# Sums of weight and activation tiles made by accumulating transfers instead of VectorE

## The chip, the cores and the metric

The kernel runs on one core of one Trainium2 chip. The metric is the device time of one execution in microseconds, as the median of repeated runs. The core has five engines with queues of their own: TensorE (PE), VectorE (DVE), ScalarE (ACT), GpSimd (POOL) and SyncE (SP), which issues transfers.

## The reference

Two layers over 1024 tokens of width 1024, all in float32. Layer 0 mixes by sliding-window attention, layer 1 by a gated linear recurrence; each is followed by a squared-ReLU block with an inner width of 4096.

```python
def sqrelu_mlp(h, w_up, w_down):
    return jnp.square(jax.nn.relu(h @ w_up)) @ w_down

for layer in range(DEPTH):
    h = rmsnorm(x, mix_norm[layer])
    y = sliding_window_attention(h, ...) if layer % N_MIXERS == 0 else hgrn2_recurrence(h, ...)
    x = x + y
    h = rmsnorm(x, mlp_norm[layer])
    x = x + sqrelu_mlp(h, mlp_w_up[layer], mlp_w_down[layer])
return rmsnorm(x, final_norm)
```

The recurrence begins with `q, f, i, g = split(h @ w_in, 4)`, four projections of 1024 by 1024.

## The kernel before, in words

All activations are held transposed, as tiles of 128 features by 512 tokens (256 KB in float32; a "half" `hf` is 512 tokens). A float32 product is made of three matmuls: each operand is split into a rounded part and a rest (`split` and `weight_split`, lines 402 and 419: a cast on ScalarE or VectorE, then a subtraction on VectorE), and `mm3` (line 384) multiplies high by high, high by low and low by high.

The up and down matrices of both layers and the four projections of the recurrence use a seven-product scheme (Strassen's, in Winograd's form). Weight and activation are cut in quarters; products 1 and 2 take plain quarters, products 3 to 7 take sums and differences of quarters on one side or both. So three kinds of sums are made, all on VectorE before the change:

- Sums of activations that stay on the chip: `begin` and `finish` (lines 508 and 516) make the seven right-hand sides of 4 tiles each once per layer. They stay on VectorE.
- Sums of weights for up and recurrence: `strassen_weights` (line 567) loads the four quarters of one group and makes four sums in "m" tiles, then splits seven tiles into "wh" and "wl" tiles. `pair` (line 581) runs the seven products for two inner tiles of the up matrix, 16 pairs per layer; `two` (line 1058) does it for two projections, twice for each of the 8 heads.
- Sums for down: `operands` (line 626) makes, for one inner tile pair `p` of 16, the weight and the activation of one product. The activations come back from HBM, where `square_relu` (line 486) had put them (`hid`). `T[p]` and `S[p]` are running sums that are kept in "a" tiles from product to product.

`down` (line 661) runs six passes over all 16 `p`: products 1 and 5, then 6, 7, 4, 2 and 3. In a pass a product of one `p` is 12 matmuls of 512 columns (4 output tiles, 3 matmuls each). Operands are asked for two steps of `p` ahead.

The order of the work is made by a planner (`Schedule`, line 140). The code says which operations there are, in which they read and write; each has a rank (its place in the code, moved ahead by `lead`), a cost and, for transfers, a tail. The planner plays the five engines forward with these costs and writes each engine's queue; a buffer of a tag ("wr" 5, "wh" 5, "wl" 5, "m" 7, "t" 18, "a" 60) is handed on when its last user has ended in that play. On the chip each queue is then worked off in order, with semaphores between the engines. Every instruction is issued by `call`, so all have one line in the profile (326 before), and groups are told apart by the tags of their tiles: `wl<-m,wh` is the rest of a split of an "m" tile.

Of the kernel before, what the change touches and what calls it, by code (L numbers as in the profile page):

```python
# [277 lines left out]
class Net:  # L278
    def __init__(self, ctx, tc, io):
# [10 lines left out]
        self.ones = self.const((P, P))  # L290
        self.memset(self.ones, 1.0)
        self.mean = self.const((P, 1))
        self.memset(self.mean, 1.0 / D)
# [102 lines left out]

    def raw(self, src):
        r = self.tile("wr", BUFS["wr"], (P, TH), F32)
        self.dma(r, src, 4 * P * TH)
        return r  # L400
# [95 lines left out]
    def gained(self, which, kt, hf):  # L496

        u = self.t()
        self.act(u, self.x[kt][hf], AF.Copy, scale=self.gain(which, kt))
        return u  # L500
# [7 lines left out]
    def begin(self, which):  # L508

        self.b, self.u = {k: [] for k in range(1, 8)}, []  # L510
        for kt in range(KT):
            u = self.gained(which, kt, 0)
            self.b[1 + kt // HK].append(self.split(u))
            self.u.append(self.keep(u))

    def finish(self, which, upper_first=False):

        x, t, q01, q11 = self.b, [], [], []

        def stored(j):  # L520
            z = self.t()
            self.dma(z, self.u[j], 4 * P * TH)
            return z

        def lower():
            for j in range(HK):
                q01.append(self.gained(which, j, 1))
                t.append(stored(j))
                self.tt("any", t[j], q01[j], t[j], ALU.subtract)
                x[5].append(self.split(t[j]))  # L530

        def upper():
            for j in range(HK):
                q11.append(self.gained(which, j + HK, 1))
                x[3].append(self.split(q11[j]))

        for part in (upper, lower) if upper_first else (lower, upper):
            part()
        for j in range(HK):
            self.tt("any", t[j], q11[j], t[j], ALU.subtract)  # L540
            x[6].append(self.split(t[j]))
        for j in range(HK):
            self.tt("any", q01[j], q11[j], q01[j], ALU.subtract)
            x[7].append(self.split(q01[j]))
        for j in range(HK):
            z = stored(j + HK)
            self.tt("any", z, z, t[j], ALU.subtract)
            x[4].append(self.split(z))
        return x
# [17 lines left out]
    def strassen_weights(self, first, second, done=()):  # L567

        self.s.lead = LEAD
        a = {(i, k): self.raw(src[:, k * TH : k * TH + TH]) for i, src in enumerate((first, second)) for k in range(2)}  # L570
# [5 lines left out]
        order = ((1, a[0, 0]), (5, s1), (2, a[0, 1]), (6, s2), (3, s4), (7, s3), (4, a[1, 1]))  # L576
        w = {name: self.weight_split(z) for name, z in order if name not in done}
        self.s.lead = 0
# [41 lines left out]

    def hidden(self, i, hf, p):
        z = self.t()
        self.dma(z, self.hid[p + i * MT // 2, hf], 4 * P * TH)
        return z

    def operands(self, name, p, T, S, held=False):

        a = lambda i, k: self.raw(self.io["down"][self.layer, k, p, :, i])
        h = lambda i, hf: self.hidden(i, hf, p)

        def sum_of(tile, x, y, alu=ALU.subtract):
            self.tt("any", tile, x, y, alu)
            return tile

        if name == 1:
            self.corner = a(0, 0), h(0, 0)
            w, x = self.corner
        elif name == 5:
            first, q00 = self.corner
            T[p] = x = sum_of(self.a(), h(0, 1), q00)  # L640
            w = sum_of(self.t(tag="m"), a(1, 0), a(1, 1), ALU.add)
        elif name == 6:
            T[p] = x = sum_of(T[p], h(1, 1), T[p])
            w = S[p]
        elif name == 7:
            x = sum_of(self.t(), h(1, 1), h(0, 1))
            w = sum_of(self.t(tag="m"), a(0, 0), a(1, 0))
        elif name == 4:
            x = sum_of(T[p], h(1, 0), T[p])
            w = a(1, 1)  # L650
        elif name == 2:
            w, x = a(0, 1), h(1, 0)
        else:
            x = h(1, 1)
            w = sum_of(S[p], a(0, 1), S[p])
        got = self.split(w) if held else self.weight_split(w), self.split(x)
        if name == 5:
            S[p] = sum_of(self.a(), w, first)
        return got

    def down(self, cut):
# [31 lines left out]

        def scaled_sum(hf, out, z, tokens=slice(0, TH)):

# [3 lines left out]
            part = out[:, tokens].only(tokens.start)  # L699
            self.tt("any", part, u, part, ALU.add, k)  # L700

# [23 lines left out]
        for i in range(2):  # L725
            for m in range(HK):
                z = residual(m + (1 - i) * HK, 1)
                scaled_sum(1, z, y[1 - i, 1, m])
                self.x[m + (1 - i) * HK][1] = z
        run_pass((4,))  # L730
        for m in range(HK):
            z = residual(m + HK, 0)
            scaled_sum(0, z, main[m])
            self.x[m + HK][0] = z
# [311 lines left out]
    def two_first(self, which, e, x):  # L1046
# [5 lines left out]
        self.product(main, w[0], x[1], True)  # L1052
        self.copy(y0, main)
        self.product(own, w[1], x[2], True)
        self.tt("DVE", y0, own, y0, ALU.add)
        return main, y0

    def two(self, which, e, x, out, begun=None):
# [6 lines left out]
        if not begun:  # L1065
            self.product(main, w[1], x[1], True)
            self.copy(y0, main)
        yield
# [3 lines left out]
        self.product(main, w[6], x[6], False)  # L1072
        self.copy(y1, main)
        yield
        if not begun:
            self.product(own, w[2], x[2], True)
            self.tt("DVE", y0, own, y0, ALU.add)
        yield
# [3 lines left out]
        self.product(side, w[3], x[3], False)  # L1082
        self.tt("DVE", y1, side, y1, ALU.add)
        yield
# [290 lines left out]
```

## Time and profile before

| | |
|---|---|
| median of 3 runs | 2181.79 us (2180.43 to 2184.33) |
| profiled execution, first to last instruction | 2174.9 us |
| PE busy | 2129.5 us (98%) |
| VectorE busy | 1823.6 us (84%) |
| ScalarE busy | 837.7 us (39%) |
| GpSimd busy | 62.4 us (3%) |
| HBM read and written | 250.39 MB and 63.96 MB, 145 GB/s over the span |

The span is of one profiled execution; what lies before the first and behind the last instruction is not in it, and the profile gives no time of its own for that execution beside the span. The stages by the rows of the trace: attention to about 342 us, the up stage of layer 0 to 653, its down stage to about 966, the recurrence with the changes of layer around it to about 1533, the second up stage to 1844, the second down stage to 2157, then the final norm.

"Busy" of PE counts matmuls that overlap in a pipeline, so a busy PE is not one at its peak; what counts is whether the next matmul had to wait. In a group's row the last columns are the busy time, the mean of one in nanoseconds, and the time that the engine stood idle just before them with what ended it. In a row of stretches there are the busy times of PE, its weight loads, DVE, ACT and POOL with their counts, the granted TensorE clock, the share of the 16 DMA engines that was busy, and the GB/s that they moved. Tile names are the tags above; `in_down` and `in_up` are weights in HBM, `d` is scratch in HBM, `p` and `q` are PSUM.

### The profile page before, as it was taken

What the parts mean: (1) busy time and instruction counts of PE and PEld (TensorE: products, weight loads), DVE (VectorE), ACT (ScalarE), POOL (GpSimd) and SP (SyncE); (2) the same over time, 40 slices, a digit from 0 to 9 for tenths busy, and PEclk for the clock granted to TensorE, in tenths of its full rate; (3) what the DMA queues carried; (4) which work ended last, traced back from release to release, by engine and by line L of the source; (5) the groups of instructions that cost most, each with busy time, mean ns of one, the idle gap of its engine ahead of it and who ended that gap; (6) DMA issues with size and microseconds to landing.
All of it is one profiled execution on the core that took longest, in us unless ns stands there. A gap on an engine that the chain in (4) does not pass through costs nothing.

```text
span 2174.9 us, 32278 instructions
## 1 busy us (share of the span) xinstructions
PE 2129.5 (98%) x11374; PEld 1713.3 (79%) x11374; DVE 1823.6 (84%) x3608; ACT 837.7 (39%) x1757; POOL 62.4 (3%) x124
## 2 busy tenths in 40 slices
PE   8999999999999999999999999999999999999997
PEld 6777778888877887877788888878788887888786
DVE  8899889667789888899888888878976678988887
ACT  5567755122234233365333333343521223322442
POOL 4030000000000000000100000000000000000000
PEclk9999999999999999999999999999999999999999
DMA  6212363333369867741111111547333336976652
GB/s 204 75 48 83 112 194 116 105 109 111 108 204 305 274 202 234 247 136 49 56 57 59 58 53 52 188 148 227 113 114 103 107 116 224 305 241 226 209 171 78
DMA packets 174274, 316.49 MB, mean 146 GB/s; under 512 B 19616, under 2 KB 21664, under 8 KB 174112
## 3 DMA queue, kind: packets, MB, share of 16 engines
q1 hardware_dynamic: 174112, 314.43, 44.7%
q8 instruction: 89, 1.46, 0.3%
q14 instruction: 73, 0.60, 0.1%
HBM read 250.39 MB, written 63.96 MB: 145 GB/s over the span
## 4 chain that ended last, share of the span: by engine, by line
PE 85%; DVE 7%; ACT 4%; DMA 2%; issue 1%; SPq 0%; DVEq 0%; ACTq 0%
PE q L326 45%; PE p L326 40%; DVE a L326 3%; DVE t L326 2%; ACT t L326 1%; ACT a L326 1%; DVE wl L326 1%; DVE m L326 1%; DMA wr<-in_down 1%; ACT m L326 1%; ACT wh L326 0%; DMA t<-d 0%; DVE wh L326 0%; DMA d<-t 0%; DMA a<-d 0%
## 5 line engine op out<-in xcount | busy, mean ns | idle before, releaser
L326 PE MATMUL q<-a,wh 128*128 128x512 f32 x2560 | 798.6, 395 | 5.0 <-DVE t L326 2.3
L326 PE MATMUL p<-a,wh 128*128 128x512 f32 x2336 | 754.4, 402 | 9.1 <-ACT t L326 3.7
L326 PEld LDWEIGHTS q<-a,wh 128*128 128x128 f32 x2560 | 480.1, 188 | 120.5 <-ACT t L326 4.1
L326 PEld LDWEIGHTS p<-a,wh 128*128 128x128 f32 x2336 | 432.0, 189 | 107.7 <-ACT t L326 4.6
L326 PE MATMUL q<-a,wl 128*128 128x512 f32 x1280 | 499.5, 394 | 0.0
L326 PE MATMUL p<-a,wl 128*128 128x512 f32 x1168 | 462.8, 397 | 0.0
L326 PEld LDWEIGHTS q<-a,wl 128*128 128x128 f32 x1280 | 240.4, 188 | 56.6
L326 PEld LDWEIGHTS p<-a,wl 128*128 128x128 f32 x1168 | 220.4, 189 | 50.5 <-issue 0.5
L326 DVE TENSOR_TENSOR wl<-wr,wh 128x512 fp32r<-128x512 f32 x352 | 241.0, 686 | 15.5 <-ACT wh L326 5.4
L326 ACT COPY t<-q 128x512 f32<-128x512 f32 (+2 forms) x201 | 111.8, 562 | 349.0 <-PE q L326 344.1
L326 DVE TENSOR_TENSOR a<-t,a 128x512 fp32r<-128x512 f32 (+1 forms) x294 | 195.0, 685 | 0.8 <-DMA t<-d 0.5
L326 DVE CAST wh<-wr 128x512 fp32r<-128x512 f32 x204 | 87.8, 430 | 127.6 <-PE p L326 78.4
L326 DVE TENSOR_TENSOR wl<-m,wh 128x512 fp32r<-128x512 f32 x256 | 176.3, 689 | 16.1 <-ACT wh L326 6.1
L326 ACT CAST wh<-m 128x512 fp32r<-128x512 f32 x153 | 95.2, 623 | 210.4 <-PE q L326 148.4
L326 DVE TENSOR_TENSOR t<-t,t 128x512 f32<-128x512 f32 (+3 forms) x268 | 159.7, 611 | 17.7 <-DMA t<-d 10.7
L326 ACT CAST a<-t 128x512 fp32r<-128x512 f32 x189 | 114.7, 619 | 128.8 <-PE q L326 82.6
L326 ACT CAST wh<-wr 128x512 fp32r<-128x512 f32 x148 | 91.1, 619 | 172.7 <-PE p L326 109.3
L326 PE MATMUL p<-wh,a 128*128 128x512 f32 x384 | 130.6, 407 | 8.2 <-ACT a L326 7.0
L326 DVE TENSOR_TENSOR m<-wr,wr 128x512 f32<-128x512 f32 x160 | 109.7, 687 | 22.2 <-DMA wr<-in_down 11.9
L326 PEld LDWEIGHTS q<-t,t 128*64 128x64 f32 (+1 forms) x2160 | 98.0, 144 | 25.0 <-issue 11.2
L326 PE MATMUL q<-t,t 128*64 128x32 f32 (+2 forms) x2160 | 111.5, 230 | 0.0
L326 DVE CAST wh<-m 128x512 fp32r<-128x512 f32 x103 | 44.3, 430 | 73.4 <-PE q L326 59.7
(117 smaller groups left out, 2113.9 us busy)
## 6 DMA issues: line engine op xcount, KB each, us to landing
t<-d SPq DMA_DIRECT2D x296, 256.0 KB, 4.7
wr<-in_down SPq DMA_DIRECT2D x256, 256.0 KB, 3.9
d<-t SPq DMA_DIRECT2D x180, 256.0 KB, 2.4
wr<-in_up SPq DMA_DIRECT2D x128, 256.0 KB, 2.9
wr<-in_win SPq DMA_DIRECT2D x68, 256.0 KB, 2.9
a<-d SPq DMA_DIRECT2D x60, 256.0 KB, 4.4
wr<-in_wqkv SPq DMA_DIRECT2D x48, 256.0 KB, 2.8
d<-a SPq DMA_DIRECT2D x48, 256.0 KB, 2.4
```

The source lines that it names most:

```text
L326: fn(*[place(a) for a in args], **{k: place(v) for k, v in kw.items()})
```

## The change

All weight sums of `strassen_weights` and all weight and activation sums of `operands` are made by transfers that GpSimd issues with `accum_op=ALU.add`: the source tile in HBM is added to a tile in SBUF that a plain transfer of SyncE had filled. In a group of weights `rows` becomes a10 + a11, then takes a00, then a01, and between the additions it is split for products 5, 6 and 3; `column` is a00 and takes a10 for product 7. In a down stage `S[p]` and `T[p]` are built in the same way over the passes, and product 7 has a pair of its own in an "m" and a "t" tile.

[...] So that all sums are additions, two quarters of the inner activations are stored negated (`square_relu` for the lower half of the inner tiles), as are two quarters of the right-hand sides (`begin`, `finish`); the splits of products 2 and 6 negate again, and signs turn where results are gathered.

```diff
+    def accumulate(self, out, in_, nbytes):
+
+        self.op("Pool", self.nc.gpsimd.dma_start, [out], [in_, out], 1100.0, out, in_, accum_op=ALU.add, tail=2500.0)
...
-    def split(self, src, new=None):
+    def split(self, src, new=None, negative=False):
         hi, lo = ((new or self.a)(F32R) for _ in range(2))
+        if negative:
+            self.act(hi, src, AF.Copy, scale=-1.0)
+            self.stt(lo, src, -1.0, hi.bitcast(F32), ALU.mult, ALU.subtract)
+            return hi, lo
...
     def square_relu(self, m, hf, c, psum):
-        r = self.t()
-        if psum:
+        r, lower = self.t(), m < MT // 2
+        if lower and not hf:
+            self.stt(r, c, 0.0, c, ALU.min, ALU.mult)
+        elif lower:
+            self.act(r, c, AF.Relu, scale=-1.0)
+            self.stt(r, c, 0.0, r, ALU.min, ALU.mult)
+        elif psum:
             self.act(r, c, AF.Relu)
-            self.stt(r, c, 0.0, r, ALU.max, ALU.mult)
+            self.stt(r, r, -1.0, r, ALU.mult, ALU.mult)
...
     def strassen_weights(self, first, second, done=()):
...
-        s1, s2, s3, s4 = (self.t(tag="m") for _ in range(4))
-        self.tt("any", s1, a[1, 0], a[1, 1], ALU.add)
-        self.tt("any", s2, s1, a[0, 0], ALU.subtract)
-        self.tt("any", s3, a[0, 0], a[1, 0], ALU.subtract)
-        self.tt("any", s4, a[0, 1], s2, ALU.subtract)
...
+        rows, column = self.raw(a[1, 0], "m"), self.raw(a[0, 0], "m")
+        self.accumulate(rows, a[1, 1], 4 * P * TH)
...
+        made(1, column)
+        made(5, rows)
+        if 2 not in done:
+            made(2, self.raw(a[0, 1]))
+        self.accumulate(rows, a[0, 0], 4 * P * TH)
+        made(6, rows)
+        self.accumulate(rows, a[0, 1], 4 * P * TH)
+        made(3, rows)
+        self.accumulate(column, a[1, 0], 4 * P * TH)
+        made(7, column)
+        made(4, self.raw(a[1, 1]))
...
         if name == 1:
-            self.corner = a(0, 0), h(0, 0)
-            w, x = self.corner
+            w, x = self.raw(a(0, 0)), self.hidden(0, 0, p)
         elif name == 5:
-            first, q00 = self.corner
-            T[p] = x = sum_of(self.a(), h(0, 1), q00)
-            w = sum_of(self.t(tag="m"), a(1, 0), a(1, 1), ALU.add)
+            T[p] = x = more_x(self.hidden(0, 1, p, self.a), 0, 0)
+            S[p] = self.a()
+            self.dma(S[p], a(1, 0), 4 * P * TH)
+            w = more_w(S[p], 1, 1)
         elif name == 6:
-            T[p] = x = sum_of(T[p], h(1, 1), T[p])
-            w = S[p]
+            w, x = more_w(S[p], 0, 0), more_x(T[p], 1, 1)
         elif name == 7:
-            x = sum_of(self.t(), h(1, 1), h(0, 1))
-            w = sum_of(self.t(tag="m"), a(0, 0), a(1, 0))
+            x = more_x(self.hidden(1, 1, p), 0, 1)
+            w = more_w(self.raw(a(0, 0), "m"), 1, 0)
         elif name == 4:
-            x = sum_of(T[p], h(1, 0), T[p])
-            w = a(1, 1)
+            w, x = self.raw(a(1, 1)), more_x(T[p], 1, 0)
...
-            x = h(1, 1)
-            w = sum_of(S[p], a(0, 1), S[p])
-        got = self.split(w) if held else self.weight_split(w), self.split(x)
-        if name == 5:
-            S[p] = sum_of(self.a(), w, first)
-        return got
+            w, x = more_w(S[p], 0, 1), self.hidden(1, 1, p)
+        return self.split(w) if held else self.weight_split(w), self.split(x, negative=name in (2, 6))
```

TensorE has the same matmuls as before. In GpSimd's queue there was no transfer before. Between the last small operation of the attention and the first of the recurrence, where the first up and down stage lie, nothing stood:

```order
L326 TENSOR_SCALAR m_2842<-c_243 128x4
L326 TENSOR_SCALAR m_2896<-c_243 128x4
L326 TENSOR_SCALAR m_2958<-c_243 128x4
L326 TENSOR_SCALAR m_3105<-c_243 128x4
L326 IOTA t_9647 128x64
```

Now the same queue at the place in the first down stage where product 7 is next. Its rows `a<-d` here add to the `T` tiles for product 4, `a<-in_down` to the `S` tiles for product 3, and `m<-in_down` to the weights of product 7:

```order
L328 DMA a_7189<-d_6540 128x512
L328 DMA a_6957<-in_down 128x512
L328 DMA a_7259<-d_6794 128x512
L328 DMA a_7039<-in_down 128x512
L328 DMA a_7135<-in_down 128x512
L328 DMA a_7200<-in_down 128x512
L328 DMA a_7270<-in_down 128x512
L328 DMA m_7850<-in_down 128x512
L328 DMA m_7874<-in_down 128x512
```

All 32 accumulations for the later products 4 and 3 stand ahead of the last nine weight sums of product 7; seven others of product 7 stand earlier, five of them among those of the up stage.

VectorE's queue in the first down stage before (`m<-wr,wr` is a sum of weights, `a<-m,wr` the running sum `S`, `a<-t,a` with a `T` tile or the rest of a split, `wl` the rest of a weight's split):

```order
L326 TENSOR_TENSOR wl_6820<-wr_6555,wh_6798 128x512
L326 TENSOR_TENSOR m_6828<-wr_6762,wr_6771 128x512
L326 TENSOR_TENSOR a_6838<-a_6796,a_6815 128x512
L326 TENSOR_TENSOR wl_6847<-m_6677,wh_6831 128x512
L326 TENSOR_TENSOR a_6852<-m_6828,wr_6738 128x512
L326 TENSOR_TENSOR a_6861<-t_6658,a_6705 128x512
```

And in the first down stage of the changed kernel:

```order
L328 CAST a_6796<-a_6684 128x512
L328 TENSOR_TENSOR wl_6801<-a_6578,wh_6785 128x512
L328 TENSOR_TENSOR a_6808<-a_6684,a_6796 128x512
L328 CAST wh_6817<-wr_6461 128x512
L328 CAST a_6821<-a_6733 128x512
L328 TENSOR_TENSOR wl_6828<-wr_6461,wh_6817 128x512
L328 TENSOR_TENSOR a_6834<-a_6733,a_6821 128x512
```

The sums are gone from it; what is left are the splits, and those of `S` and `T` tiles (`a_6578`, `a_6684`, `a_6733`) now follow a transfer of GpSimd.

More of the change, by code (lines that the diff above doesn't have):

```diff
@@ L395, in gain, with neg_gain, raw @@
         return self.par[:, which * KT + kt : which * KT + kt + 1]
-    def raw(self, src):
-        r = self.tile("wr", BUFS["wr"], (P, TH), F32)
+    def neg_gain(self, which, kt):
+        return self.neg_par[:, which * KT + kt : which * KT + kt + 1]
+    def raw(self, src, tag="wr"):
+        r = self.tile(tag, BUFS[tag], (P, TH), F32)
         self.dma(r, src, 4 * P * TH)
@@ L692, in run_pass, with scaled_sum @@
             return ws
-        def scaled_sum(hf, out, z, tokens=slice(0, TH)):
+        def scaled_sum(hf, out, z, tokens=slice(0, TH), add=True):
             k = tokens.stop - tokens.start
@@ L699, in scaled_sum @@
             part = out[:, tokens].only(tokens.start)
-            self.tt("any", part, u, part, ALU.add, k)
+            self.tt("any", part, part, u, ALU.add if add else ALU.subtract, k)
         def residual(m, hf):
@@ L1052, in two_first @@
         self.product(main, w[0], x[1], True)
-        self.copy(y0, main)
+        self.act(y0, main, AF.Copy, scale=-1.0)
         self.product(own, w[1], x[2], True)
-        self.tt("DVE", y0, own, y0, ALU.add)
+        self.tt("DVE", y0, y0, own, ALU.subtract)
         return main, y0
@@ L1076, in two @@
             self.product(own, w[2], x[2], True)
-            self.tt("DVE", y0, own, y0, ALU.add)
+            self.tt("DVE", y0, y0, own, ALU.subtract)
         yield
@@ L1082, in two @@
         self.product(side, w[3], x[3], False)
-        self.tt("DVE", y1, side, y1, ALU.add)
+        self.tt("DVE", y1, y1, side, ALU.subtract)
         yield
```

50 lines of the change are left out of this document (28 added, 22 removed).

## The prediction

> **What bounds the kernel now.** I read the page first: engines, DMA queues, then the chain of work that ended last.
>
> ```profile
> span 2174.9 us, 32278 instructions
> ...
> PE 2129.5 (98%) x11374; PEld 1713.3 (79%) x11374; DVE 1823.6 (84%) x3608; ACT 837.7 (39%) x1757; POOL 62.4 (3%) x124
> ...
> q1 hardware_dynamic: 174112, 314.43, 44.7%
> ...
> PE 85%; DVE 7%; ACT 4%; DMA 2%; issue 1%; SPq 0%; DVEq 0%; ACTq 0%
> ...
> L326 DVE TENSOR_TENSOR m<-wr,wr 128x512 f32<-128x512 f32 x160 | 109.7, 687 | 22.2 <-DMA wr<-in_down 11.9
> ```
>
> The chain is TensorE for 85% and VectorE for 7%. VectorE is busy (84%) but mostly beside TensorE. A busy PE need not be a full one, so the second view is the chain in order of time. A piece of it from the first up stage (columns: start, length, what):
>
> ```profile
> 383.66 16.67 PE q L326 x72
> ```
>
> 72 matmuls of 512 columns in 16.67 us are 0.232 us each, with nothing between. The third view cuts the span into stages (columns: busy time of PE, PEld, DVE, ACT, POOL, granted clock, DMA share, GB/s). The first three down rows are the passes for products 1 and 5, for 6, and for 7:
>
> ```profile
> 342.00:653.00 311.00, 310.96 (x1343) 251.19 (x1342) 234.22 (x406) 79.07 (x141) 0.00 (x0) 1.00 0.39 125
> 653.00:742.00 89.00, 88.16 (x382) 71.19 (x381) 82.28 (x138) 33.39 (x58) 0.00 (x0) 1.00 0.92 304
> 742.00:787.00 45.00, 45.00 (x196) 36.52 (x195) 36.75 (x67) 11.42 (x20) 0.00 (x0) 1.00 0.47 148
> 787.00:832.00 45.00, 44.71 (x194) 35.85 (x193) 41.28 (x71) 16.08 (x30) 0.00 (x0) 1.00 0.86 292
> ...
> 921.00:966.00 45.00, 41.79 (x174) 33.52 (x173) 40.49 (x99) 28.48 (x53) 0.36 (x2) 0.92 0.49 158
> 966.00:1010.00 44.00, 40.70 (x170) 31.85 (x169) 41.51 (x79) 26.17 (x48) 0.00 (x0) 0.96 0.17 58
> 1010.00:1490.00 480.00, 475.93 (x3866) 384.22 (x3865) 418.28 (x955) 177.04 (x364) 9.70 (x18) 1.00 0.29 92
> ...
> 1844.00:1933.00 89.00, 87.56 (x378) 70.58 (x377) 83.00 (x139) 33.09 (x57) 0.00 (x0) 1.00 0.91 305
> ```
>
> Two things are to be seen. In every stage that the change touches, TensorE is idle for a few microseconds at most. And the DMA engines, nearly idle in the recurrence, are at 0.92 in the first down pass and 0.86 in the pass for product 7. The kernel is bound by TensorE, with the transfers of the down stage close behind.
>
> **Part 1: what VectorE loses.** The sums that go: 4 for each of 32 up pairs (128), 4 for each of 16 calls in the recurrence layer (64), and 8 for each of 32 inner tiles of the two down stages (256). 448 sums by 687 ns are 308 us of VectorE. Off the path it is worth what TensorE idles for it, so I bound the gain by TensorE's idle time in the rows above: 3.2 us (921 to 966), 3.3 (966 to 1010), 4.1 (1010 to 1490), 0.8 and 1.4 in the two first down passes: 12.8 us in all. The up stage, with 128 of the sums, can give nothing (310.96 of 311). Part of the idle time is the change of layer, where other vector work remains. I take 8 us, between 0 and 12.8.
>
> **Part 2: what the other engines get.** No matmul is added or removed. ScalarE alone now negates the splits of products 2 and 6 (64 casts that could go to either engine) and gets 32 more activations in the up stages. At 39% busy it hides them; it would have to be over twice as busy before they cost anything. One 128x64 VectorE operation at the start is nothing. Signs turned inside other operations leave their count as it was.
>
> **Part 3: what the DMA engines get.** The up and recurrence stages keep their four plain loads per group and gain four accumulating transfers, which read the source and also the tile that is added to. At shares of 0.39 and 0.29 there is room. In a down stage the 16 loads per inner tile become 10 plain loads and 8 accumulations. No row shows the price of an accumulation, so I bound it in units of a plain 256 KB transfer. Below: one unit, if reading back the tile costs nothing. Above: two, since it reads 512 KB where a load reads 256. By all bytes read and written (768 KB against 512) it is 1.5. I take 1.75, the middle of the last two.
>
> A unit's time comes from stretches where the engines were full:
>
> ```profile
> 690.00:695.00 5.00, 5.00 (x24) 4.05 (x23) 4.99 (x10) 2.31 (x5) 0.00 (x0) 1.00 0.98 346
> 810.00:815.00 5.00, 5.00 (x24) 4.07 (x23) 4.90 (x9) 0.66 (x2) 0.00 (x0) 1.00 1.06 395
> ```
>
> 346 GB/s at a share of 0.98 is 353 GB/s when full, so 262,144 bytes take 0.743 us. The best stretch (395) gives 0.664, the page's whole queue (314.43 MB in 44.7% of 2174.9 us, 323 GB/s) 0.81.
>
> Now the deadline. The GpSimd order has seven kinds of accumulation in a down stage: two each for products 5, 6 and 7, one each for 4 and 3. Those for 4 and 3 stand ahead of the last nine weight sums of product 7, because these nine wait for the seven "m" buffers. So by the time TensorE wants the eighth inner tile of product 7, 16 times 7 and 3 more accumulations must have landed: 115 (five of product 7's weight sums are made in the up stage). Beside them are 83 plain loads: 32 for product 1, 32 for product 5, 19 for product 7. TensorE arrives there after 384 + 192 + 84 = 660 matmuls, 153 us. The last up pair frees its "a" buffers from its first product on, so transfers start some 16.7 us earlier (72 matmuls). I take off 3 us for the split of the tile. That leaves 167 us.
>
> The sum for one down stage, (83 + 115 f) by 0.743 us: for f = 1, 147 us, which fits; for f = 1.75, 211 us, 44 us late; for f = 2, 233 us, 66 late. Later passes need few transfers and cannot win anything back, since TensorE has no slack. Two stages at f = 1.75: 89 us lost. The median of the runs, 2181.8, is 6.9 us above the profiled span; I take that as constant. 2181.8 + 89 - 8 = 2263.
>
> The waits that come with it: a split on VectorE or ScalarE waits for the accumulation's landing, and behind it in the same queue stand the splits of other tiles and the copies out of PSUM, so a late accumulation holds more than its own product.
>
> A rule speaks against the change too. The Trainium skill, Collectives: The Full Stack, section "The bandwidth ceiling: the fold count and why AG ≠ RS ≠ AR", says that a reducing transfer ran at about half the rate of a copy, because the add needs two source reads (62.28 against 32.35 GB/s, a ratio of 1.93). No run here shows it yet. By that ratio as an estimate the sum would be 305 units, 227 us, 60 us late, and the time 2293.
>
> **The rivals.** First, accumulations cost hardly more than loads, f below 1.2: everything lands in time (147 us against 167), TensorE stays the bound, and the gain of part 1 is left: 2181.8 - 8 = 2174. For it: the read-back is of SBUF, not of HBM, and the share of 0.47 in product 6's pass shows that transfers can be spread. Against it: even f = 1 fills 147 of 167 us, where before had a share of (0.92 x 89 + 0.47 x 45 + 0.86 x 19) / 153 = 0.78 over the three passes up to there.
>
> Second, GpSimd's issue becomes the bound. All 115 are issued by one queue in order, so it decides from 167 / 115 = 1.45 us each. The rows of GpSimd (the last columns: busy us, mean ns) lie on both sides:
>
> ```profile
> L326 POOL MEMSET t<- 64x256 f32 (+2 forms) x32 | 12.1, 384 | 457.8 <-PE p L326 358.4 <-DVE t L326 70.7 <-PE q L326 28.4
> ...
> L326 POOL TENSOR_SCALAR a<-t 128x512 f32<-128x512 f32 x2 | 4.8, 2413 | 25.0 <-issue 18.5 <-DVE t L326 6.5
> ```
>
> At 0.38 us nothing happens; at 2.41 us, an operation on a tile of this very size, 115 take 277 us, 111 late in each stage: 2181.8 + 221 - 8 = 2395. What could raise the price is VectorE. Its casts take 430 ns where the sums take 687:
>
> ```profile
> L326 DVE CAST wh<-wr 128x512 fp32r<-128x512 f32 x204 | 87.8, 430 | 127.6 <-PE p L326 78.4
> ```
>
> The Trainium skill, SBUF — State Buffer, section "Who interferes with whom", says that descriptor writing for GpSimd's transfers is shut out while VectorE runs in a mode that takes both ports, and copies and casts can enter it. The trace agrees that casts run in a faster mode; it shows no GpSimd transfer that they could hold up.
>
> That accumulations are merely late, one by one, I don't count as a case: up groups have five "wh" buffers (five products, 13.9 us) of lead, and a plain load of "up" lands in 2.9 us:
>
> ```profile
> wr<-in_up SPq DMA_DIRECT2D x128, 256.0 KB, 2.9
> ```
>
> **How the numbers follow.** Transfers bound the first three down passes: 0.54. TensorE stays the bound: 0.35, of which 0.10 stays within 0.2% (about what a measurement of this kernel can tell from no change, 4.4 us) since the gain has 0 as its lower end, and 0.25 is faster by more. GpSimd's issue bounds: 0.11. So faster 0.25, same 0.10, slower 0.65. The likeliest case's own range: f = 1.25 at 0.743 us is 2 us late per stage, 2177 in all; f = 2 at 0.81 us is 87 late, 2347. The range has to take in part of the first rival: from 2173 to 2350; it leaves out the best gains and GpSimd's upper price, together some 2 in 10.
>
> **What would show it.** Right: in the profile of the changed kernel the DMA share is near 1 from just before the first down pass to the middle of product 7's, TensorE is idle there by tens of microseconds, VectorE's and ScalarE's splits wait for GpSimd's transfers into "a" and "m", and a 256 KB accumulation takes well over one unit of engine time; the up stages still last 311 us. First rival: TensorE full in all down passes, share below 1, and the gain is found at the layer's change and in the recurrence. Second: GpSimd's accumulations follow one another at 1.5 us or more without a wait while the DMA share stays low. Wrong altogether: an up stage longer than 311 us, since I gave the up stages nothing, or idle time that begins after product 7.

## The result and the profile after

The changed kernel takes 2304.78 us (median of 4 runs, 2300.1 to 2312.36); the kernel before took 2181.11 us beside it (4 runs, 2180.27 to 2184.33). The ratio is 1.0567, with an interval of 1.0541 to 1.0592: slower by 124 us. The forecast was slower by 81 us.

From the page of the kernel after: span, engines, the two DMA queues (packets, MB, share of 16 engines), the chain by engines, a group of GpSimd's transfers, VectorE's cast, and the median time from issue to landing.

```profile
span 2307.5 us, 32855 instructions
...
PE 2165.5 (94%) x11374; PEld 1729.3 (75%) x11374; DVE 1617.4 (70%) x3308; ACT 777.4 (34%) x1644; POOL 457.6 (20%) x572
...
q1 hardware_dynamic: 146176, 263.56, 34.5%
q0 software_dynamic: 64512, 117.47, 30.5%
...
PE 41%; DMA 6%; DVE 3%; issue 2%; ACT 1%; POOL 0%; SPq 0%; DVEq 0%; POOLq 0%; ACTq 0%
...
L328 DVE CAST wh<-wr 128x512 fp32r<-128x512 f32 x216 | 93.0, 431 | 94.9 <-PE p L328 50.1
...
L328 POOL DMA_DIRECT2D a<-in_down x96 | 105.5, 1170 | 63.7 <-DMA a<-in_down 27.4
...
m<-in_up POOLq DMA_DIRECT2D x128, 256.0 KB, 5.0
...
a<-d POOLq DMA_DIRECT2D x96, 256.0 KB, 9.7
a<-in_down POOLq DMA_DIRECT2D x96, 256.0 KB, 9.7
```

All matmuls are still there and VectorE is 206 us less busy, yet the span is 132.6 us longer. (The medians differ by 124 us only: a timed execution takes about 2 us more than its span, so the profiled execution of before, 2174.9 us, was faster than its median, and that of after, 2309.25 us timed, slower.)

The queue q0 is new: it holds the 448 accumulations, and for 117 MB it takes nearly as much engine time as q1 for 264 MB. Divided by its count, an accumulation takes 30.5% of 2307.5 us / 448 = 1.57 us of all 16 engines; a plain 256 KB takes 34.5% of 2307.5 us / 1005 = 0.79 us (263.56 MB are 1005 times 256 KB). By these packet times the price is 1.98 units over the whole execution. From 657 to 780 us, where the DMA engines were full all the time, the queues give another count:

```profile
q0 software_dynamic: 7771, 14.16, 63.1%
q1 hardware_dynamic: 10562, 19.23, 45.0%
```

These are 54.0 accumulations and 73.4 plain transfers in 123 us. At the forecast's 0.743 us for a plain one, 68.5 us are left, 1.27 us or 1.7 units for an accumulation; at 0.664 us, its best stretch, 2.1. The two shares add up to 1.08, so packet times overlap and are not exact prices. The price lies between 1.7 and 2.1 units, and no run fixes it closer.

The stages of the kernel after, with the columns of the forecast's table (the last row is the first pass of the second down stage):

```profile
342.00:653.00 311.00, 303.49 (x1299) 242.25 (x1298) 178.81 (x329) 69.71 (x123) 56.27 (x63) 1.00 0.66 160
653.00:742.00 89.00, 59.91 (x217) 44.94 (x216) 41.67 (x76) 13.12 (x23) 35.00 (x40) 0.85 1.07 272
742.00:787.00 45.00, 28.52 (x104) 21.69 (x103) 11.41 (x22) 3.00 (x5) 19.12 (x23) 0.84 1.09 255
787.00:832.00 45.00, 43.80 (x183) 35.09 (x182) 28.86 (x52) 13.03 (x22) 31.58 (x36) 0.96 1.11 209
...
1920.00:2048.00 128.00, 93.49 (x335) 70.18 (x334) 46.59 (x85) 15.15 (x26) 53.76 (x61) 0.86 1.10 265
```

Before, 382 matmuls ran between 653 and 742 us; now 217. The DMA engines are full (1.07, 1.09) and move less than the 304 GB/s of before, since much of their time goes to accumulations. GpSimd works 35 of 89 us: it is not full. TensorE's granted clock falls to 0.85 while it stands and starts. The up stage lost some too: 303.5 of 311.

The next view is the waits of the kernel after between 653 and 787 us (engine and tile, what it waited for: us in all, times, longest):

```profile
ACT a L328 <- DMA a<-d: 75.5, 8, 22.2
DVE a L328 <- DMA a<-d: 49.4, 8, 13.7
POOL a L328 <- DMA a<-d: 32.2, 8, 10.3
...
PEld q L328 <- DVE wh L328: 17.5, 4, 8.5
PEld q L328 <- ACT t L328: 17.4, 4, 8.5
```

The splits wait for transfers of activations, up to 22 us; TensorE waits for the splits, and also for the copies out of PSUM ("t") that stand behind them in ScalarE's queue.

To place the loss I numbered TensorE's matmuls, took the start of each in a trace less its start in the trace of before, and give how much this lateness grew in each stage (us; the marks are 342, 653, 742, 787, 832, 966, 1533, 1844, 1933, 1978 and 2023 us of the trace of before; P1/5 is the pass for products 1 and 5, "rest" the passes for 4, 2 and 3, and what follows). Each row is of one profiled execution. That of before was some 4 us faster than its median, and every row carries this: e3, with the time of before, adds up to 3 us.

| kernel | to 342 | up | P1/5 | P6 | P7 | rest | recurrence | up | P1/5 | P6 | P7 | rest |
|---|---|---|---|---|---|---|---|---|---|---|---|---|
| after | 2.3 | 29.9 | 42.6 | -0.1 | -0.6 | -3.4 | 5.4 | 14.1 | 43.4 | -0.1 | -1.0 | -0.1 |
| e1 | 2.2 | 3.1 | -0.9 | -0.1 | 2.7 | 0.3 | 6.6 | 4.8 | -1.7 | -0.1 | 2.1 | 2.0 |
| e2 | 0.4 | 10.4 | 45.2 | -0.1 | -0.7 | -0.8 | 2.1 | 8.0 | 46.8 | 0.0 | -1.1 | 0.0 |
| e3 | 2.7 | 0.2 | -0.9 | -0.1 | 0.8 | 0.6 | 2.9 | -1.2 | -1.7 | -0.1 | 0.5 | -0.2 |
| e4 | 2.3 | 12.8 | 11.6 | -0.1 | -0.6 | -3.4 | 5.6 | 5.9 | 11.0 | -0.1 | -1.0 | -0.1 |
| e5 | 3.3 | 10.7 | 12.6 | -0.1 | -0.6 | -3.4 | 6.0 | 11.8 | 14.4 | -0.1 | -1.0 | -0.5 |
| e7 | 1.3 | 0.7 | 0.0 | -0.1 | 0.5 | 0.4 | 1.8 | -1.4 | -0.9 | -0.1 | 1.4 | 2.0 |
| e8 | 1.2 | 5.4 | 25.8 | -0.1 | 11.4 | -2.5 | 1.3 | 5.4 | 23.7 | -0.1 | 11.3 | 1.7 |
| e10 | 1.3 | 0.1 | -0.9 | 27.4 | 4.9 | -0.5 | 2.0 | -0.5 | -1.9 | 28.8 | 5.6 | 1.9 |
| e11 | 2.6 | 0.0 | -0.9 | 22.1 | 7.6 | -2.3 | 2.5 | -0.3 | -1.9 | 23.1 | 6.7 | 2.8 |
| e12 | 1.0 | 8.4 | 22.8 | -0.1 | 10.0 | -0.4 | 1.5 | 4.9 | 23.7 | -0.1 | 8.3 | 1.3 |
| e13 | 2.7 | -0.4 | -0.9 | -0.1 | 5.4 | 3.7 | 2.3 | -0.4 | -2.0 | -0.1 | 4.3 | 2.3 |
| e14 | 0.9 | 6.2 | 23.6 | -0.1 | -0.6 | -1.3 | 2.0 | 5.2 | 23.4 | 0.0 | -0.9 | 0.5 |

The loss of a down stage falls in its first pass, before TensorE asks for product 6, and at the end of the up stage ahead of it. That is not the place that the forecast named, the eighth inner tile of product 7.

In GpSimd's queue the reason can be counted. The planner lets the accumulations for products 6 and 7 in between those for product 5: the last weight sum of product 5 is the 64th accumulation of a down stage (32 for product 5, 26 for product 6, 6 for product 7; five more of product 7, sent during the up stage, are not counted). In front of it 88 plain loads go out too, some 70 of them in the time that the forecast's way of counting covers. At two units, (70 + 2 x 64) by 0.743 us are 147 us; by the forecast's way of counting, 16.7 + 15/16 of 89 - 3 = 97 us are at hand. So 50 us late, as an estimate. Measured were 43 in each first pass, and with the end of the up stage ahead some 55 (e2's row, 10.4 + 45.2 and 8.0 + 46.8, where the up stage has no accumulations of its own). Whether this place in the queue decides is put to the test in e8.

### The profile page after: what moved, and what is told of

Same layout as the page of the kernel before. It is cut to its first block, busy times and chain, and to the rows that moved or that the text cites. A ratio compares the mean times of both kernels' runs of the same rounds, so it can differ in the third digit from the quotient of the medians.

```text
span 2307.5 us, 32855 instructions
## 1 busy us (share of the span) xinstructions
PE 2165.5 (94%) x11374; PEld 1729.3 (75%) x11374; DVE 1617.4 (70%) x3308; ACT 777.4 (34%) x1644; POOL 457.6 (20%) x572
## 3 DMA queue, kind: packets, MB, share of 16 engines
q1 hardware_dynamic: 146176, 263.56, 34.5%
q0 software_dynamic: 64512, 117.47, 30.5%
## 4 chain that ended last, share of the span: by engine, by line
PE 41%; DMA 6%; DVE 3%; issue 2%; ACT 1%; POOL 0%; SPq 0%; DVEq 0%; POOLq 0%; ACTq 0%
PE q L328 22%; PE p L328 19%; DMA a<-d 4%; DMA t<-d 1%; DVE t L328 1%; DVE a L328 1%; ACT t L328 0%; DMA m<-in_win 0%; DVE wl L328 0%; DMA a<-in_down 0%; DMA m<-in_up 0%; DMA d<-t 0%; DVE m L328 0%; DVE wh L328 0%; SPq L328 0%
## 5 line engine op out<-in xcount | busy, mean ns | idle before, releaser
L328 PE MATMUL q<-a,wh 128*128 128x512 f32 x2560 | 814.4, 401 | 69.4 <-ACT t L328 34.9
L328 PE MATMUL p<-a,wh 128*128 128x512 f32 x2336 | 758.2, 403 | 10.4 <-ACT wh L328 5.6
L328 POOL DMA_DIRECT2D m<-in_up x128 | 114.1, 1001 | 636.6 <-DVE wl L328 437.4
L328 DVE CAST wh<-m 128x512 fp32r<-128x512 f32 x198 | 85.3, 431 | 205.3 <-DMA m<-in_up 109.1
L328 DVE TENSOR_TENSOR wl<-wr,wh 128x512 fp32r<-128x512 f32 x306 | 209.8, 687 | 11.0 <-ACT wh L328 1.4
L328 ACT CAST a<-t 128x512 fp32r<-128x512 f32 x153 | 92.4, 619 | 233.0 <-PE q L328 84.5
L328 POOL DMA_DIRECT2D m<-in_win x64 | 55.4, 870 | 469.9 <-DVE wl L328 245.1
L328 DVE TENSOR_TENSOR a<-t,a 128x512 fp32r<-128x512 f32 (+1 forms) x198 | 133.6, 689 | 8.7 <-ACT a L328 5.5
L328 DVE TENSOR_TENSOR t<-t,t 128x512 f32<-128x512 f32 (+2 forms) x212 | 122.8, 594 | 8.7 <-ACT t L328 5.6
L328 POOL DMA_DIRECT2D a<-d x96 | 99.2, 1165 | 133.3 <-DMA a<-d 54.9
L328 POOL DMA_DIRECT2D a<-in_down x96 | 105.5, 1170 | 63.7 <-DMA a<-in_down 27.4
L328 PEld LDWEIGHTS q<-t,t 128*64 128x64 f32 (+1 forms) x2160 | 98.3, 144 | 25.7 <-PE p L328 12.8
```

Of the source, the lines that this page charges most:

```text
L328: fn(*[place(a) for a in args], **{k: place(v) for k, v in kw.items()})
```

## The experiments

**Which sums cost.** In e1 the sums of the down stage are made by VectorE again, from a plain load and an addition (`added`); in e2 those of up and recurrence; in e3 all of them, so that the changed signs alone are left.

```diff
+    def added(self, out, in_, nbytes, tag="wr"):
+        u = self.t(tag=tag)
+        self.dma(u, in_, nbytes)
+        self.tt("any", out, out, u, ALU.add)
...
@@ e1: operands @@
-            self.accumulate(tile, a(i, k), 4 * P * TH)
+            self.added(tile, a(i, k), 4 * P * TH)
...
-            self.accumulate(tile, self.hid[p + i * MT // 2, hf], 4 * P * TH)
+            self.added(tile, self.hid[p + i * MT // 2, hf], 4 * P * TH, "t")
@@ e2: strassen_weights, all four of this kind @@
-        self.accumulate(rows, a[1, 1], 4 * P * TH)
+        self.added(rows, a[1, 1], 4 * P * TH)
```

e3 has both edits.

> The changed kernel with the 256 sums of the two down stages made by VectorE again (plain load, then an addition, in the changed signs); up and recurrence keep their 192 accumulations. Theory A (accumulations take two units of DMA engine time, 1.57 us against 0.79 in the changed kernel's queues, and overfill the first three down passes): both down stages are as before, and only the 10 us of the first up stage and the change of layer are left: 2185 to 2195 us. Rival D (the cost lies in what came with the signs: negating splits, added activations): stays near 2305.

> The opposite half: sums of up and recurrence by VectorE, the down stages keep their 256 accumulations. Theory A: 2181 + 65 + 57 = about 2300 us (2292 to 2306), the loss all in the first three passes of each down stage, DMA share near 1.1 there. If up's accumulations did the harm by filling the transfers ahead of the down stage, the first down stage is clearly shorter than in the changed kernel and the time is below 2285.

> All 448 sums by VectorE, in the changed signs: what the signs and the two loads more per inner tile cost by themselves. Theory A: 2181 within 5 us, since TensorE bounds and ScalarE hides the negations. Rival D: well above, 2200 or more.

The kernel before took 2181.63 us beside these three and e4. Measured: e1 2199.23 us, ratio 1.0072 (1.005 to 1.0094); e2 2285.51 us, 1.0465 (1.0444 to 1.0486); e3 2181.09 us, 0.9998 (0.9986 to 1.0011). So the signs and ScalarE's added work cost nothing, and of the 124 us the down stages hold 104 and the 192 sums of up and recurrence 18. That last term I had put at nothing. (e1 is 4 us above the range that was expected of it, and e2 some 7 below its range.) e2 shows too that 8 to 10 us of a down stage's loss fall at the end of the up stage ahead of it, where the first accumulations of down are sent.

**The price: the addition or the transfer.** In e4 the 256 transfers of the down stages lack the addition; in e5 they add half of the columns.

```diff
@@ e4 @@
+    def copied(self, out, in_, nbytes):
+        self.op("Pool", self.nc.gpsimd.dma_start, [out], [in_, out], 1100.0, out, in_, tail=2500.0)
...
-            self.accumulate(tile, a(i, k), 4 * P * TH)
+            self.copied(tile, a(i, k), 4 * P * TH)
...
-            self.accumulate(tile, self.hid[p + i * MT // 2, hf], 4 * P * TH)
+            self.copied(tile, self.hid[p + i * MT // 2, hf], 4 * P * TH)
@@ e5 @@
-            self.accumulate(tile, a(i, k), 4 * P * TH)
+            self.accumulate(tile[:, : TH // 2], a(i, k)[:, : TH // 2], 2 * P * TH)
...
-            self.accumulate(tile, self.hid[p + i * MT // 2, hf], 4 * P * TH)
+            self.accumulate(tile[:, : TH // 2], self.hid[p + i * MT // 2, hf][:, : TH // 2], 2 * P * TH)
```

> The changed kernel with the addition left out of the down stages' 256 accumulating transfers: GpSimd issues plain copies of the same bytes into the same tiles, in the same order, with the same waits; the sums are not made. Theory A: a copy takes one unit, (83 + 115) x 0.79 = 156 us of the 167 at hand, so the down stages are as before: 2185 to 2200 us. Rival B (GpSimd's issue, 0.86 us each and in order, and the place of the transfers in its queue): stays at 2290 to 2310. Rival C (the round trip of each transfer, some 3 us or more whatever its kind, in a chain of load, addition and split): most of the loss stays, above 2260.

> The changed kernel with each accumulation of the down stages over the first 256 of the 512 columns only (half of each sum is left out): the same 256 GpSimd transfers with the same waits and the same order, each with half the bytes and so about the DMA engine time of one plain transfer. Theory A: as with the copies, 2215 to 2235 us. Rivals B and C (issue, order or round trip of each transfer): nothing of that is halved, so 2280 or more.

Measured: e4 2226.30 us, ratio 1.0197 (1.0165 to 1.0228); e5 2229.85 us, 1.0224 (1.0202 to 1.0246; the kernel before 2181.95 us beside it). First the row of e4 between 653 and 742 us, then that of e5 and e5's rows on GpSimd (busy us, mean ns):

```profile
653.00:742.00 89.00, 76.45 (x303) 60.02 (x302) 45.59 (x85) 14.00 (x24) 32.71 (x60) 0.92 1.01 368
```

```profile
653.00:742.00 89.00, 74.43 (x294) 57.96 (x295) 42.62 (x79) 13.89 (x24) 51.66 (x59) 0.92 1.08 271
...
L328 POOL DMA_DIRECT2D a<-in_down x96 | 131.2, 1694 | 46.0 <-DVE wl L328 21.5 <-DMA a<-in_down 13.1 <-PE q L328 3.9
```

With the addition gone the same count of GpSimd transfers loses 45 us in place of 124, so the addition is worth 78. Half of the bytes is worth 75. Copying made GpSimd's instructions shorter too (0.55 us), so e4 by itself leaves open whether GpSimd's time was the cost. e5 doesn't: there, as in after, GpSimd's instructions that follow one another directly end 0.89 us apart (median), so each takes as much of GpSimd as before, and GpSimd is busy 51.66 of the 89 us against 35.00 in after; yet the loss is less than half. (The longer mean, 1694 ns against 1170, shows only that more of them stood in line, since their records overlap.) What the transfers move sets it. e5 came out as theory A expected; e4 met none of the three expectations and lies between A's 2200 and C's 2260. About 18 of its 45 us are those of e1; the other 27 and e5's 30 are a remainder: e4's share of 1.01 in the first pass says that even plain transfers, in this order, leave the DMA engines no room there. By the count above, with one unit each, (70 + 64) by 0.743 us are 100 for 97 at hand, 3 us late per stage as an estimate; some 13 were lost. Nothing was run that tells the count of the transfers from their order.

**The 18 us of up and recurrence.** e7 is e1 with one number changed: the planner is told that an accumulation lands 5.0 us after its issue (the page's median), not 2.5.

```diff
-        self.op("Pool", self.nc.gpsimd.dma_start, [out], [in_, out], 1100.0, out, in_, accum_op=ALU.add, tail=2500.0)
+        self.op("Pool", self.nc.gpsimd.dma_start, [out], [in_, out], 1100.0, out, in_, accum_op=ALU.add, tail=5000.0)
```

> The kernel with only up's and recurrence's accumulations (down by VectorE, 2199 us), with one number of the planner changed: it takes an accumulation to land 5.0 us behind its issue cost, where it took 2.5. In the trace of the changed kernel they land 5.0 us from the issue, and ScalarE stood 102 us before splits of such tiles with copies out of PSUM queued behind. Theory Q (the 18 us come from splits placed too early in the queues, not from the DMA engines): 2181 to 2188 us. Rival (transfer load, share 0.64 to 0.72 in up stages, or VectorE and GpSimd shutting each other out): stays at 2193 to 2203.

Measured: 2182.54 us, ratio 1.0003 (0.9988 to 1.0018): the 18 us are gone. The waits of e1, then of e7, between 342 and 653 us:

```profile
ACT wh L328 <- DMA m<-in_up: 46.7, 15, 4.6
...
DVE wh L328 <- DMA m<-in_up: 42.2, 15, 4.3
```

```profile
ACT wh L328 <- DMA m<-in_up: 31.8, 15, 4.5
...
DVE wh L328 <- DMA m<-in_up: 7.0, 5, 2.3
```

The accumulations are the same and as many. In e1 the planner believed them there in 2.5 us, put the splits early into the queues of ScalarE and VectorE, and these stood still (47 and 42 us) with the copies out of PSUM behind them. With the right landing time it puts other work first. That the copies behind cost the 18 us is argued: against e3's row, e1's loses 9 us at the ends of the two up stages and none before, and the rest in the recurrence and from product 7 on, while the waits shown are those of the first up stage as a whole. What e7 shows is that the planner's landing time sets the loss, and not the load on the DMA engines. e7 has another lesson: 192 sums less on VectorE, and it is no faster than the kernel before.

**The order in the down stage.** e8 is the kernel after with the planner's cost of an accumulation at the measured 1.57 us and the landing at 5.0 us; nothing else is touched. So the change of e7 is in it too, and the order within the down stage is to be read from the first passes.

```diff
-        self.op("Pool", self.nc.gpsimd.dma_start, [out], [in_, out], 1100.0, out, in_, accum_op=ALU.add, tail=2500.0)
+        self.op("Pool", self.nc.gpsimd.dma_start, [out], [in_, out], 1570.0, out, in_, accum_op=ALU.add, tail=5000.0)
```

> The changed kernel, all accumulations kept, with the planner's price of one set to what the trace shows: 1.57 us instead of 1.1, landing 5.0 us later instead of 2.5. GpSimd's order changes: the last weight sum of product 5 is its 46th transfer of a down stage instead of the 64th. Theory A: what stands before it is (64 + 46 x 2) x 0.743 = 116 us for 97 at hand, so the first pass loses some 19 us instead of 43, and product 7's pass now loses the rest, since its last weight sum has 107 accumulations and some 91 loads ahead, 227 us for 187: about 37 us per stage in all, 2250 to 2270 us. If order were everything and engine time nothing: below 2200. If order were nothing: 2295 to 2310.

Measured: 2262.33 us, ratio 1.0373 (1.035 to 1.0396), 42 us better than after. The last weight sum of product 5 is now the 46th accumulation in GpSimd's queue, not the 64th: (70 + 2 x 46) by 0.743 us is 120 us, 23 late. The first passes lose 25.8 and 23.7 us in place of 42.6 and 43.4, with the ends of the up stages 31 and 29. New are 11 us in each pass for product 7; e14 shows what they are. In the row between 653 and 742 us TensorE has 261 matmuls, against 217:

```profile
653.00:742.00 89.00, 67.79 (x261) 52.42 (x260) 40.32 (x76) 11.14 (x19) 33.78 (x39) 0.90 1.09 285
```

**Only the late products.** The passes for 4, 2 and 3 have a slack of DMA. So in e10 only the sums for products 4 and 3 (64 of 256) are accumulations, and all others are VectorE's.

```diff
+            (self.added if name in (5, 6, 7) else self.accumulate)(tile, a(i, k), 4 * P * TH)
...
+            self.added(tile, *more, "t") if name in (5, 6, 7) else self.accumulate(tile, *more)
```

> Only the sums of products 4 and 3 in the down stages by accumulation (64 of 448), where the DMA share before was 0.13 to 0.68; all others by VectorE. Theory A: no stall, TensorE bounds, and VectorE's 44 us less buy at most the idle time around the change of layer: 2176 to 2184 us, most likely the same as before.

Measured: 2243.33 us, ratio 1.0281 (1.0263 to 1.03; the kernel before 2181.95 us beside it). That refuted my reading: 64 accumulations cost 61 us. The pass for product 6, first in e3 (none of these accumulations), then in e10:

```profile
742.00:787.00 45.00, 45.00 (x197) 36.58 (x196) 44.09 (x77) 15.09 (x28) 0.00 (x0) 1.00 0.89 311
```

```profile
742.00:787.00 45.00, 29.74 (x115) 22.47 (x113) 24.29 (x40) 9.46 (x17) 14.41 (x17) 0.88 1.10 289
```

The loss is in the pass for product 6 (27 us), two passes before product 4 and four before product 3. GpSimd's column shows why: it is at work there (17 operations), though the sums are for products 4 and 3. Their tile stands already and is free as soon as product 6 has been split; nothing else holds GpSimd back, so it sends them at once into a stage whose DMA share is 0.89 without them.

**Holding them back.** e11 is e10 with a dependency that only the planner knows: an accumulation counts as reading a plain tile of its own pass. e12 does the same to e8. e13 is e10 with a real wait: GpSimd first reads four columns of that plain tile. e14 is e8 with the real wait for the sums of products 4 and 3.

```diff
@@ e11; e12 the same with 1570.0 and tail=5000.0 @@
-        self.op("Pool", self.nc.gpsimd.dma_start, [out], [in_, out], 1100.0, out, in_, accum_op=ALU.add, tail=2500.0)
+        self.op("Pool", self.nc.gpsimd.dma_start, [out], [in_, out, behind], 1100.0, out, in_, accum_op=ALU.add, tail=2500.0)
@@ e13, e14: ahead of the transfer @@
+        if behind is not None:
+            seen = self.t(F32, (P, 4), "sm")
+            self.op("Pool", self.nc.gpsimd.tensor_scalar, [seen, out], [behind], 350.0, seen, behind[:, :4], 1.0, None, ALU.mult)
```

> The same 64 accumulations as in the run with products 4 and 3 alone (2243 us), but in the planner's order each stands behind a plain load of its own pass, so that GpSimd issues it in the pass for 4 or 3 and not in the pass for 6 or 7. Not one transfer, byte or VectorE operation differs. Theory A, with the addition that what counts is when GpSimd's queue issues them: no stall, 2177 to 2186 us, the same as before. If something about these accumulations themselves cost the 61 us (their latency, their place between two splits of one tile): 2225 or more.

> All 448 accumulations, the planner's price as in the run before it with a price of 1.57 us (2262 us), and those for products 4 and 3 held in the same way to their own passes. Theory A: the first pass still loses some 25 us per stage, since nothing ahead of product 5's last sum changed, and the 11 to 13 us at product 7 go, since fewer accumulations stand ahead of its last weight sums: 2235 to 2250 us. If the loss were only one of order, it would go on falling to below 2220.

> The run before this one did not do what it was meant to: a place in GpSimd's queue is no wait, the queue held nothing else, and its trace shows GpSimd's transfers between 742 and 832 us, in the passes for products 6 and 7, as in the run with 4 and 3 alone. Now GpSimd itself waits: ahead of each of the 64 accumulations it reads 4 columns of the plain tile that product 4 or 3 of the same inner tile loads (64 small operations more). Theory A: the transfers leave the passes for 6 and 7 and the loss goes, 2177 to 2188 us. If these accumulations cost the time by themselves, wherever they are: 2225 or more.

> All 448 accumulations with the planner's price of 1.57 us (2262 us), those for products 4 and 3 held in the same real way. Theory A: the first pass loses its 25 us per stage as before (nothing ahead of product 5's last sum changed), the 10 us at product 7 go or become few: 2235 to 2250 us. If order were all: below 2220.

Measured: e11 2234.46 us, ratio 1.0242 (1.0228 to 1.0256); e12 2260.00 us, 1.0366 (1.0347 to 1.0385), which is e8's time (the kernel before 2179.91 us beside these two); e13 2192.36 us, 1.0047 (1.0033 to 1.0061); e14 2237.84 us, 1.0262 (1.0241 to 1.0284; the kernel before 2180.46 us beside these two). e11 and e12 did not do what was meant: a planner's dependency moves the place in the queue, and a place in the queue is no wait. The passes for products 6 and 7 in e11, then in e13:

```profile
742.00:787.00 45.00, 38.65 (x157) 29.80 (x156) 33.93 (x57) 12.58 (x23) 13.95 (x19) 0.96 1.08 328
787.00:832.00 45.00, 35.34 (x129) 26.44 (x129) 24.79 (x45) 8.97 (x15) 10.30 (x12) 0.89 0.99 246
```

```profile
742.00:787.00 45.00, 45.00 (x197) 36.61 (x196) 43.23 (x76) 14.99 (x27) 0.00 (x0) 1.00 0.87 304
787.00:832.00 45.00, 45.00 (x196) 36.52 (x195) 36.48 (x65) 11.87 (x21) 10.28 (x11) 1.00 0.83 244
```

In e11 GpSimd still sends 19 operations in the pass for product 6; in e13 none, the share there is 0.87, and TensorE is full again. The loss goes from 61 us (e10) to 12 (e13) with the same 64 accumulations; e13 was expected to lose none, and is 4 us above its range. In e14 the 11 us of e8 at product 7 are gone (-0.6, -0.9): they came from the sums of products 4 and 3, sent too early. The 23 us of the first passes stay, since those sums were not held.

No kernel of these beats the one before: e3 and e7 equal it.

## Why the forecast was right, and where it was not

**What bounds the kernel: right.** TensorE before, and the transfers of the first down passes after: share near 1 from just before the first pass, splits waiting for GpSimd's transfers into "a", TensorE idle by tens of microseconds.

**Part 1, VectorE's sums, 8 us: too much.** e7 takes 192 sums off VectorE and is at 1.0003; e3 has them all and is at 0.9998. For these 192 the term is nothing. For the 256 of down no run shows it by itself: the kernel after gained 3.4 us in the first stage's pass for product 3 and lost 2.6 at the change of layer, where the forecast looked for some of it, and nothing of the kind is seen in the second. VectorE did not get 308 us freer either, but 206: it has 300 instructions fewer and not 448, since others came to it, and ScalarE has 113 fewer.

**Part 2, signs and ScalarE: right that they cost nothing.** e3 is the whole of it. ScalarE ended with less work, not with more: 777 us against 838.

**Part 3, the price, 1.75 units: low, but not by more than its own uncertainty.** By packet times it is 1.98 over the kernel after and 1.81 in e2 (down alone: 16.4% of 2284.8 us / 256 = 1.46 us against 0.81); by what the full engines moved it is 1.7 to 2.1. The Trainium skill, Collectives: The Full Stack, section "The bandwidth ceiling: the fold count and why AG ≠ RS ≠ AR", gives a ratio of 1.93 between AllGather and ReduceScatter over four ranks; here, for an addition from HBM into a tile of the same core, 1.98 by packet times roughly agrees. With 1.98 the forecast's sum gives 231 us, 64 late per stage, and with 1.75 it gave 44. Measured per stage were 52 to 57 (e2: half of 104; the table of after: 43 and what of the up stage's end is down's).

**Part 3, the deadline: right in kind, wrong in place.** I took the eighth inner tile of product 7 as the point where it decides. (The 115 accumulations up to there are right, though the text names eight kinds and counts seven: 112 are all those but product 7's weight sums, of which 3 more are needed.) The order of GpSimd's queue makes it the last tile of product 5, with 64 accumulations ahead; no loss is left at product 7, since the transfers of products 6 and 7 came in that time. e8, where 46 stand ahead and the first pass loses 25, bears this out. Its 11 us at product 7 show that the forecast's point was a limit as well, hidden behind the earlier one. At the forecast's own price the right point gives (70 + 1.75 x 64) by 0.743 = 135 us, 38 late, where the wrong one gave 44. That the two have about the same excess is luck, and it is why the sum for down came near. The range, 2173 to 2350, held a gain as well as a loss of 168 us; that the time lies in it says little.

**The up stages, nothing: wrong by 18 us.** I had named a longer up stage as what would show me wrong, and it is 7.5 us short of work by 653 us. I had dismissed accumulations that are "merely late" by the buffers' lead of 13.9 us. With the same buffers e7 loses nothing, so what did not cover them is the order in the queues. The forecast had the mechanism in its sentence on the waits (a late accumulation holds what is queued behind it) and gave it no price. e7 shows that it hung on one number of the planner.

**The rivals.** That accumulations cost hardly more than loads is refuted by 1.98. GpSimd's issue as the bound is refuted too: in the first pass GpSimd is busy 35 of 89 us, and in e5 it spends as much on each transfer and the loss is smaller. Where it has several in a row, it ends one each 0.89 us (timeline of after, start and length of GpSimd's transfers):

```profile
666.25 0.86 POOL L328 DMA_DIRECT2D a<-d  x1 [10.26 <-DMA a<-d]
666.94 1.06 POOL L328 DMA_DIRECT2D a<-in_down  x1
667.59 1.31 POOL L328 DMA_DIRECT2D a<-d  x1
```

They end at 667.11, 668.00 and 668.90 us. The rows overlap, so the mean of 1170 ns is not the pace; 0.89 us is far below the 1.45 us at which that rival would have decided. Before the first of them it waited 10.26 us for a plain load to land. VectorE does hold GpSimd up, as the forecast feared, but little: of the transfers of after that start when no other is in work, the 202 without a cast of VectorE beside them took 0.86 us in the mean and 0.92 at most, the 108 beside a cast 0.90 and 1.16.

**Adding up.** 104 us in down and 18 in up and recurrence make 122 of the 124 measured. The forecast's 81 were 89 for down, less 8 for VectorE, so it fell short by 15 in down, 18 in up and recurrence and 8 for VectorE. It set the median against the profiled span with 6.9 us as constant; only some 2 of them are, and the rest is that this execution was a fast one. The sum starts from the median, so nothing hung on it.

**Open.** How much of the down stages' loss in e4 and e5 (27 and 30 us) is the count of transfers and how much their order; e13's last 12 us, which lie at products 7 and 4; by which waits the 18 us of e1 reach TensorE; and why an accumulating packet takes twice as long. That the second read does it is argued, not shown.

## What to carry to other kernels

Count a transfer that adds as nearly two, and set it against the room that the DMA engines have in that very stage, not over the whole span: the work leaves an engine that was off the path and lands on one that was nearly full. When an order is planned, the deadline is where the last transfer that a pass needs stands in its queue, with all that was let in ahead of it; and the landing time that the planner believes must be the measured one. A place in a queue holds nothing back: transfers into tiles that stand ready go out at once, and only a real wait keeps them for a later stage.

## What the runs showed of the hardware

- In the trace of after, a packet of 2 KB took 178 ns (median) when it was added and 84 ns when it was only written; with 1 KB (e5) an added one took 102 ns.
- Where GpSimd's transfers only copy (e4), they were cut into packets of 4 KB (queue q0 then holds 48,128 packets in place of 64,512), at 166 ns each, and those into "a" landed in 5.5 to 5.7 us where the accumulations took 9.7.
- In stretches where TensorE stands every few microseconds, its granted clock fell to 0.84 to 0.92, so that a part of the loss is slower matmuls: between 653 and 742 us 217 matmuls took 59.9 us of busy time, and at 0.232 us each would have taken 50.3.
- VectorE's casts took 431 ns in the kernel with the 448 transfers of GpSimd and 430 in the one without. A transfer of GpSimd with an addition took 0.86 us of GpSimd alone, and up to 1.16 us beside such a cast; one that only copies took 0.54 us at the least.
- GpSimd's queue held no transfer back by its order: those of e10 and e11 for products 4 and 3 went out in the passes for 6 and 7, and with a real wait ahead of each (e13) none went out in the pass for product 6.
